# Rotary keys' low part: from 64 to 128 partitions

## The chip, the cores and the metric

The kernel runs on one core of one Trainium2 chip. The metric is the device time of one launch in microseconds (us). In the text, PE is TensorE (the matmul engine), DVE is VectorE, ACT is ScalarE, POOL is GpSimd, and SP the engine that issues most of the DMAs. SBUF and PSUM are the on-chip memories; matmuls write to PSUM. "Partitions" are the 128 rows of these memories, and for the two operands of a matmul they are the rows over which it sums.

## What is computed

Two layers over 512 latent tokens of width 1024, with 256 context tokens beside them. Layer 0 is a latent attention with 8 heads followed by a squared-ReLU MLP, layer 1 a gated MLP that mixes positions in chunks, followed by a second squared-ReLU MLP. The change lies in the attention's scores. Queries and keys have 128 entries without position and 64 rotary ones; the rotary part of the keys is one vector per token, shared by the heads, and only scaled by each head's norm:

```python
def mla_keys_values(h, wkv_a, kv_a_norm, wkv_b, k_norm):
    ...
    k_pe = jnp.broadcast_to(k_pe[:, :, None, :], (B, S, MLA_HEADS, QK_ROPE))
    k = rmsnorm(jnp.concatenate([k_nope, k_pe], axis=-1), k_norm)
    return k, v

def block_attention(q, k, v, scale):
    ...
        s = jnp.einsum('bqhd,bkhd->bhqk', qi, k, preferred_element_type=jnp.float32) * scale
        p = jax.nn.softmax(s, axis=-1)
        return jnp.einsum('bhqk,bkhd->bqhd', p.astype(v.dtype), v)
```

## The kernel before

Everything is float32 in memory, and matmuls run in a faster reduced form of it (`F32R`). To keep the precision, an operand is split in two: a high part, which is the value rounded to that form, and a low part, which is the rest (`split`, lines 70 to 77: ACT writes the high part, DVE or POOL subtracts). A product is then three matmuls: high by high, high by low, low by high (`mm3`, lines 79 to 82).

The attention goes head by head. For each head, `kv_proj` makes keys and values of all 768 tokens, `q_proj` makes the queries of two heads, `scores` makes the softmax of a half of the query tokens, `values` transposes the probabilities and multiplies them with the values, and `out_proj` multiplies the result with the output weights. These pieces are interleaved by a list of steps (`fill`), and the scheduler of the framework then sets the order on each engine; between `scores` and the `values` that use them lies other work, since the scores of a step are made one step ahead.

The rotary part of the queries is kept as one tile `sq` per head of 128 partitions: the high part on partitions 0 to 63 and the low part on 64 to 127, stacked. The rotary keys are transposed twice over, so that the same 64 rows stand on both halves of the PSUM tile `krt` (lines 536 to 541). From there ACT writes `rh`, the high part, on all 128 partitions (line 543), so that one product of `sq` with `rh` gives high by high plus low by high. DVE writes `rl`, the low part (line 544), on 64 partitions, and it is multiplied with partitions 0 to 63 of `sq` alone.

A score block, which is one pass through the loop on line 634, makes the scores of 128 queries of one head against 768 keys. It adds five products in PSUM (tile `s`, one buffer of two banks), each as two matmuls of 384 columns: ten matmuls on line 640. There are 32 blocks, 320 matmuls. A matmul here is two instructions on PE: one loads the stationary operand (`lhsT`, here the queries) into the array, listed as PEld, and one streams the other operand through it. A block's end releases DVE, which scales the scores and takes their maximum (line 644), then ACT the exponential (line 647), then DVE the division (line 649). The next block can't start before line 644 has read the tile.

While the attention runs, POOL also accumulates the modulation vectors (`ada_steps`, lines 169 to 172) from weights that it fetches itself.

Of the kernel before, what the change touches and what calls it, by code (L numbers as in the profile page):

```python
# [9 lines left out]
F32 = mybir.dt.float32  # L10
F32R = mybir.dt.float32r
BF16 = mybir.dt.bfloat16
AF = mybir.ActivationFunctionType
ALU = mybir.AluOpType
AX = mybir.AxisListType

P = 128
# [4 lines left out]
TOK = CTX + SEQ  # L22
# [4 lines left out]
ROPE = 64  # L27
# [19 lines left out]
def hybrid_dit_kernel(  # L47
# [7 lines left out]
    PE, ACT, DVE, POOL = nc.tensor, nc.scalar, nc.vector, nc.gpsimd  # L55
    SBUF, PSUM = bass.MemoryType.SB, bass.MemoryType.PSUM

    def pool(stack, name, bufs=1, space=SBUF, side="left"):
        return stack.enter_context(tc.tile_pool(name=name, bufs=bufs, space=space, side=side, reuse_waits="tile"))
# [157 lines left out]
    ap_ = pool(att, "att")  # L217
# [2 lines left out]
    cq_h = ap_.tile([P, 3, SEQ], F32R, name="cq_h")  # L220
    cq_l = ap_.tile([P, 3, SEQ], F32R, name="cq_l")
    rh = ap_.tile([P, TOK], F32R, name="rh")
    rl = ap_.tile([ROPE, TOK], F32R, name="rl")
    epk = ap_.tile([P, NT], F32, name="epk")
    cosT = ap_.tile([P, NT, ROPE], F32, name="cosT")
    sinT = ap_.tile([P, NT, ROPE], F32, name="sinT")
# [112 lines left out]
    with ExitStack() as ini_stack:  # L339
# [7 lines left out]
        def pt(name):  # L347
            return ps.tile([P, 512], F32, tag="t", bufs=2, name=name)

        def pa(name):  # L350
            return ps.tile([P, 512], F32, tag="a", bufs=6, name=name)
# [60 lines left out]
        with ExitStack() as xstack:  # L412
# [12 lines left out]
            for k in range(0, KT, 2):  # L425
                o = pa(f"xct{k}")
# [4 lines left out]
            for k in range(KT):  # L431
                o = pa(f"xt{k}")
# [7 lines left out]
        for t in range(NT):  # L440
            o = rp[0][:, t * P:(t + 1) * P] if t < 2 else rp[1][:, (t - 2) * P:(t - 1) * P]
# [18 lines left out]
        for k in range(KT):  # L460
# [6 lines left out]
            for t in range(NT):  # L467
                a_h, a_l = (ch, cl) if t < 2 else (hh[k], hl[k])
                s = bass.ts(t if t < 2 else t - 2, P)
# [23 lines left out]
        for t in range(NT):  # L493
# [8 lines left out]
            o = pt(f"ckt{t}")  # L502
            for j in range(2):
                PE.transpose(o[:, j * P:(j + 1) * P], ck[:, j * P:(j + 1) * P], ident)
            for j in range(2):
                s = slice(t * P, (t + 1) * P)
# [12 lines left out]
        for t in range(NL):  # L519
            o = pa(f"qa{t}")  # L520
            for k in range(KT):
                s = bass.ts(t, P)
# [15 lines left out]
        for u in range(2):  # L538
            o = pt(f"krt{u}")
            for j in range(3):  # L540
                PE.transpose(o[:, j * P:(j + 1) * P], kpe[:, 3 * u + j, :, :].rearrange("p a r -> p (a r)"), ident)
            s = slice(u * 384, (u + 1) * 384)
            ACT.copy(out=rh[:, s], in_=o[:, :384])
            DVE.tensor_tensor(out=rl[:, s], in0=o[:ROPE, :384], in1=rh[:ROPE, s].bitcast(F32), op=ALU.subtract)

        drain(kv0)

# [63 lines left out]
    with hst as st_:  # L611
# [17 lines left out]
        def scores(h, half):  # L629
            kh, kl, rk = Ks[h]  # L630
            rk = rk.rearrange("p (a b) -> p a b", a=2)
            qh, ql, sq, rq_ = Qs[h // 2]
            i = h % 2
            for t in (2 * half, 2 * half + 1):
                s = slice(t * P, (t + 1) * P)
                S = ps.tile([P, 2, 512], F32, tag="s", bufs=PS, name=f"s{h}{t}")
                ops = [(qh[:, i, s], kh), (qh[:, i, s], kl), (ql[:, i, s], kh), (sq[i][:, s], rh), (sq[i][:ROPE, s], rl)]
                for m, (a, b) in enumerate(ops):
                    for n in range(2):
                        PE.matmul(S[:, n, :384], lhsT=a, rhs=b[:, n * 384:(n + 1) * 384], start=m == 0, stop=m == 4)  # L640
                sm = hq.tile([P, 4], F32, tag="sm", bufs=4, name=f"sm{h}{t}")
                rq = rq_[:, t, i, 2:3]
                e = hq.tile([P, 2, 384], F32, tag="p", bufs=5, name=f"p{h}{t}")
                DVE.tensor_tensor_reduce(out=e, in0=S[:, :, :384], in1=rk, op0=ALU.mult, op1=ALU.max, scale=rq,  # L644
                                         scalar=-3.0e38, accum_out=sm[:, 0:1])
                DVE.tensor_scalar(out=sm[:, 1:2], in0=sm[:, 0:1], scalar1=-1.0, scalar2=None, op0=ALU.mult)  # L646
                ACT.activation(out=e, in_=e, func=AF.Exp, bias=sm[:, 1:2], accum_out=sm[:, 2:3])  # L647
                DVE.reciprocal(out=sm[:, 3:4], in_=sm[:, 2:3])
                DVE.tensor_scalar(out=e, in0=e, scalar1=sm[:, 3:4], scalar2=None, op0=ALU.mult)  # L649
                Pr[h, t] = e.rearrange("p a b -> p (a b)")  # L650
# [47 lines left out]
        drain(q_proj(0)); ada_step(8)  # L698
        steps = [(h, half) for h in range(HEADS) for half in range(2)]
        scores(0, 0)  # L700
        drain(kv_proj(1))
        fill = {}
# [7 lines left out]
        for i, (h, half) in enumerate(steps):  # L710
            if i + 1 < len(steps):
                scores(*steps[i + 1])
            values(h, half)
            ada_step(ADS[i])
            for g, n in fill.get((h, half), []):
                drain(g, n)
            if i == len(steps) - 2:
                out_last(3, 0)
# [117 lines left out]
    with ExitStack() as st_:  # L836
# [7 lines left out]
        for q in range(4):  # L844
            ws = [W(gm_w_in, 2 * k2, 2, HALF + q * 512, 512, f"gv{q}{k2}") for k2 in range(4)]
            for ts in ((0, 1), (2, 3)) if q == 0 else ((0, 1, 2, 3),):
                acc = {t: (pu if t < 2 else pd)(f"v{q}{t}") for t in ts}
                for k in range(KT):
                    wh, wl = ws[k // 2]
                    for t in ts:  # L850
                        s = slice(t * P, (t + 1) * P)
# [11 lines left out]
        for g4 in range(2):  # L863
            o = pt(f"wst{g4}")
# [6 lines left out]
            o = pt(f"rsw{g4}")  # L871
# [121 lines left out]
```

## Time and profile before

| | us |
|---|---|
| median of three runs | 1432.6 |
| the three runs | 1427.57, 1432.6, 1439.05 |
| the profiled execution | 1433.93 |
| its span (first to last instruction) | 1431.8 |
| PE busy in the span | 1370.9 (96%) |
| DVE busy | 872.3 (61%) |
| ACT busy | 547.3 (38%) |
| POOL busy | 243.8 (17%) |

The profile is that of one execution. A matmul's duration in it is the time from its start to a modelled end; matmuls overlap, so durations add up to more than the engine's time, and the distance from one start to the next tells the pace. A weight load (PEld) can overlap the matmul ahead of it. An idle stretch is given as "[0.25 <-issue]": so many us before the instruction, and what ended it, where "issue" means nothing that the profile shows. The granted clock is the share of the full clock of 2.4 GHz that PE had; 0.50 is 1.2 GHz.

### The profile page before, as it was taken

What the parts mean: (1) busy time and instruction counts of PE and PEld (TensorE: products, weight loads), DVE (VectorE), ACT (ScalarE), POOL (GpSimd) and SP (SyncE); (2) the same over time, 40 slices, a digit from 0 to 9 for tenths busy, and PEclk for the clock granted to TensorE, in tenths of its full rate; (3) what the DMA queues carried; (4) which work ended last, traced back from release to release, by engine and by line L of the source; (5) the groups of instructions that cost most, each with busy time, mean ns of one, the idle gap of its engine ahead of it and who ended that gap; (6) DMA issues with size and microseconds to landing.
All of it is one profiled execution on the core that took longest, in us unless ns stands there. A gap on an engine that the chain in (4) does not pass through costs nothing.

```text
span 1431.8 us, 18446 instructions
## 1 busy us (share of the span) xinstructions
PE 1370.9 (96%) x7159; PEld 1160.1 (81%) x7159; DVE 872.3 (61%) x1367; ACT 547.3 (38%) x1046; POOL 243.8 (17%) x262
## 2 busy tenths in 40 slices
PE   6887989999979999999999999999999999999998
PEld 4686878997868888888889788888888888888888
DVE  4766788778789988753456536555476344343443
ACT  6544654664454133231334423222245233242331
POOL 4467174173051111000000001000020000000000
PEclk9997999999989999999999999999999999999999
DMA  8523032131157888623232323222222233323311
GB/s 275 168 83 111 16 98 67 40 111 52 37 170 238 277 269 266 207 96 103 88 104 89 103 81 105 95 88 74 89 89 89 88 103 99 93 89 91 101 59 60
DMA packets 126823, 163.23 MB, mean 114 GB/s; under 512 B 7467, under 2 KB 111488, under 8 KB 126736
## 3 DMA queue, kind: packets, MB, share of 16 engines
q1 hardware_dynamic: 114784, 119.50, 26.4%
q0 software_dynamic: 11808, 42.03, 9.1%
q8 instruction: 56, 0.92, 0.3%
q10 hardware_dynamic: 144, 0.52, 0.1%
q14 instruction: 31, 0.25, 0.1%
HBM read 159.94 MB, written 2.10 MB: 113 GB/s over the span
## 4 chain that ended last, share of the span: by engine, by line
PE 86%; DVE 6%; ACT 2%; issue 1%; POOL 0%; DMA 0%; ACTq 0%; DVEq 0%; POOLq 0%
PE s L640 4%; PE v L80 2%; PE v L82 2%; PE v L81 2%; PE pt L662 1%; PE wo L80 1%; PE f1d2o L81 1%; PE f1d0o L80 1%; PE f1d0o L82 1%; PE f1d2o L82 1%; PE f1d2o L80 1%; PE f1d0o L81 1%; PE f0d0o L80 1%; PE f0d1o L80 1%; PE f0d1o L81 1%
## 5 line engine op out<-in xcount | busy, mean ns | idle before, releaser
L166 DVE SCALAR_TENSOR_TENSOR acc<-adr,sil,acc 128x1024 f32<-128x1024 f32 x49 | 62.8, 1281 | 9.5 <-DMA adr<-in_ada_w_dram 8.9
L161 POOL DMA_DIRECT2D adr<-in_ada_w_dram x80 | 44.0, 550 | 142.3 <-DVE acc L166 86.7
L172 POOL TENSOR_TENSOR acc<-acc,adr 128x512 f32<-128x512 f32 x42 | 55.7, 1343 | 0.2
L169 POOL TENSOR_TENSOR adr<-adr,sil 128x512 f32<-128x512 f32 x42 | 45.4, 1100 | 19.0 <-DMA adr<-in_ada_w_dram 19.0
L789 DVE TENSOR_TENSOR f1a<-f1a 128x512 f32<-128x512 f32 (+1 forms) x36 | 22.5, 629 | 41.3 <-ACT f1a L788 41.3
L644 DVE CUSTOM_DVE_ANT_0 p<-s,rk,rq 128x768 f32<-128x768 f32 x32 | 32.4, 1014 | 15.9 <-PE s L640 15.8
L126 POOL TENSOR_TENSOR nst<-nst,mhalf 128x2 f32<-128x2 f32 x6 | 4.6, 765 | 209.3 <-DVE nst L125 209.3
L73 DVE TENSOR_TENSOR tl<-pt,th 128x512 fp32r<-128x512 f32 x48 | 32.5, 685 | 11.3 <-ACT th L72 11.1
L72 ACT CAST f0uh<-f0a 128x512 fp32r<-128x512 f32 (+1 forms) x36 | 20.6, 573 | 48.5 <-DVE f0a L789 48.3
L789 DVE TENSOR_TENSOR f0a<-f0a 128x512 f32<-128x512 f32 (+1 forms) x36 | 22.6, 628 | 24.8 <-ACT f0a L788 24.8
L647 ACT ACTIVATE p<-p,sm 128x768 f32<-128x768 f32 x32 | 30.1, 940 | 15.6 <-DVE sm L646 15.4
L72 ACT CAST th<-pt 128x512 fp32r<-128x512 f32 x48 | 27.6, 588 | 20.2 <-PE o L82 11.6
L73 DVE TENSOR_TENSOR f1ul<-f1a,f1uh 128x512 fp32r<-128x512 f32 (+1 forms) x36 | 22.6, 631 | 18.7 <-ACT f1uh L72 18.5
L73 POOL TENSOR_TENSOR f1u00w01l<-f1u00w01r,f1u00w01h 128x1024 fp32r<-128x1024 f32 x1 | 2.4, 2390 | 182.0 <-ACT f1u00w01h L72 182.0
L72 ACT CAST f1uh<-f1a 128x512 fp32r<-128x512 f32 (+1 forms) x36 | 20.5, 572 | 32.8 <-DVE f1a L789 32.8
L81 PE MATMUL o<-tl,vh 128*128 128x256 f32 x96 | 28.5, 297 | 1.7 <-DVE tl L73 1.6
L73 DVE TENSOR_TENSOR f0ul<-f0a,f0uh 128x512 fp32r<-128x512 f32 (+1 forms) x36 | 22.6, 628 | 11.7 <-ACT f0uh L72 11.7
L649 DVE TENSOR_SCALAR p<-p,sm 128x768 f32<-128x768 f32 x32 | 29.0, 905 | 0.8
L80 PE MATMUL o<-th,vh 128*128 128x256 f32 x96 | 28.8, 300 | 0.0
L662 PE MATMUL pt<-ident,p 128*128 128x128 f32 x192 | 28.3, 276 | 0.0
L607 DVE SCALAR_TENSOR_TENSOR xT<-wo,mod,xT 128x512 f32<-128x512 f32 (+1 forms) x40 | 25.1, 638 | 4.0 <-PE wo L82 3.9
L82 PE MATMUL o<-th,vl 128*128 128x256 f32 x96 | 27.1, 282 | 0.0
(2640 smaller groups left out, 4815.3 us busy)
## 6 DMA issues: line engine op xcount, KB each, us to landing
adr<-in_ada_w_dram POOLq DMA_DIRECT2D x80, 512.0 KB, 4.8
xn<-in_x_dram SPq DMA_DIRECT2D x4, 512.0 KB, 7.1
out_dram<-of SPq DMA_DIRECT2D x8, 256.0 KB, 2.1
xn<-in_ctx_dram SPq DMA_DIRECT2D x2, 512.0 KB, 4.3
ada000r<-in_ada_w_dram SPq DMA_DIRECT2D x1, 512.0 KB
ada001r<-in_ada_w_dram SPq DMA_DIRECT2D x1, 512.0 KB
ada100r<-in_ada_w_dram SPq DMA_DIRECT2D x1, 512.0 KB, 11.2
ada101r<-in_ada_w_dram SPq DMA_DIRECT2D x1, 512.0 KB, 10.0
```

The lines of the kernel that those rows point to most:

```text
L72: ACT.copy(out=hi, in_=src)
L73: eng.tensor_tensor(out=lo, in0=src, in1=hi.bitcast(F32), op=ALU.subtract)
L80: PE.matmul(o, lhsT=wh, rhs=mh, start=start, stop=False)
L81: PE.matmul(o, lhsT=wh, rhs=ml, start=False, stop=False)
L82: return PE.matmul(o, lhsT=wl, rhs=mh, start=False, stop=stop)
L161: nc.gpsimd.dma_start(out=r, in_=ada_w[l][k * P:(k + 1) * P, ch * D:(ch + 1) * D])
L166: DVE.scalar_tensor_tensor(out=acc, in0=r, scalar=sil[:, k, 0:1], in1=acc, op0=ALU.mult, op1=ALU.add)
L169: POOL.tensor_tensor(out=(acc if k == 0 else r)[:, hf], in0=r[:, hf], in1=sil[:, k, 0:1].to_broadcast([P, D // 2]), op=ALU.mult)
L172: POOL.tensor_tensor(out=acc[:, hf], in0=acc[:, hf], in1=r[:, hf], op=ALU.add)
L640: PE.matmul(S[:, n, :384], lhsT=a, rhs=b[:, n * 384:(n + 1) * 384], start=m == 0, stop=m == 4)
L662: PE.transpose(T[:, j, q * P:(q + 1) * P], Pr[h, 2 * half + q][:, (2 * jp + j) * P:(2 * jp + j + 1) * P], ident)
L789: DVE.tensor_tensor(out=f, in0=f, in1=f, op=ALU.mult)
```

## The change

The tile `rl` gets 128 partitions instead of 64. The subtraction that fills it takes all partitions of the transposed tile and of `rh`, so the same 64 rows of low parts stand on both halves. The fifth product of a score block takes the whole stacked query tile with it, so that it sums over 128 rows instead of 64: high by low plus low by low, the last of which was not computed before.

```diff
-    rl = ap_.tile([ROPE, TOK], F32R, name="rl")
+    rl = ap_.tile([P, TOK], F32R, name="rl")
...
-            DVE.tensor_tensor(out=rl[:, s], in0=o[:ROPE, :384], in1=rh[:ROPE, s].bitcast(F32), op=ALU.subtract)
+            DVE.tensor_tensor(out=rl[:, s], in0=o[:, :384], in1=rh[:, s].bitcast(F32), op=ALU.subtract)
...
-                ops = [(qh[:, i, s], kh), (qh[:, i, s], kl), (ql[:, i, s], kh), (sq[i][:, s], rh), (sq[i][:ROPE, s], rl)]
+                ops = [(qh[:, i, s], kh), (qh[:, i, s], kl), (ql[:, i, s], kh), (sq[i][:, s], rh), (sq[i][:, s], rl)]
```

Every engine has the same number of instructions as before, in the same order; only the two subtractions and the 64 matmuls on `rl`, with their loads, have another shape.

## Rows read from the trace of the kernel before

**Rows 1.** Page, part 1: busy us, share of the span, instructions.

```profile
PE 1370.9 (96%) x7159; PEld 1160.1 (81%) x7159; DVE 872.3 (61%) x1367; ACT 547.3 (38%) x1046; POOL 243.8 (17%) x262
```

**Rows 2.** Stretches: length; PE, PEld, DVE, ACT, POOL busy (instructions); clock; DMA; GB/s.

```profile
142.00:380.00 238.00, 227.12 (x1438) 200.99 (x1439) 185.40 (x388) 130.67 (x370) 96.27 (x87) 0.98 0.20 62
182.40:185.60 3.20, 3.20 (x12) 3.20 (x11) 2.26 (x8) 2.25 (x7) 2.47 (x4) 0.50 0.41 118
```

**Rows 3.** Stretches, line 640 alone: length; PE, PEld busy (instructions); clock; DMA; GB/s.

```profile
142.00:380.00 238.00, 70.16 (x312) 51.44 (x312) 0.98 0.20 62
180.00:220.00 40.00, 9.26 (x42) 7.03 (x43) 0.91 0.28 88
300.00:340.00 40.00, 9.32 (x40) 6.34 (x38) 0.96 0.29 93
```

**Rows 4.** Chain that ended last, 142 to 380 us: shares by line; one piece.

```profile
by line: PE s L640 23.1%; PE pt L662 6.9%; PE wo L80 5.4%; PE wo L81 4.6%; PE wo L82 4.5%; PE o L81 4.2%; PE o L80 3.9%; PE kv L80 3.7%; PE o L82 3.7%; PE rkb L283 3.5%; PE kv L81 3.3%; PE kv L82 3.2%; PE q L80 2.6%; PE q L81 2.5%; PE q L82
...
375.59 1.94 PE s L640 x10
```

**Rows 5.** Waits of PE, 142 to 380 us: us in total, times, longest.

```profile
PE q L80 <- DVE qg L311: 2.9, 1, 2.9
```

**Rows 6.** Line 640 by operand: ns min/median/max, first and last start us.

```profile
L640 PEld LDWEIGHTS s<-rh,sq x64: 187/188/237, 141.2 to 376.5; 128*128 128x128 f32 x64
L640 PE MATMUL s<-rh,sq x64: 334/338/424, 141.4 to 376.6; 128*128 128x384 f32 x64
L640 PEld LDWEIGHTS s<-rl,sq x64: 182/183/187, 141.8 to 377.0; 64*128 64x128 f32 x64
L640 PE MATMUL s<-rl,sq x64: 327/436/442, 141.8 to 377.2; 64*128 64x384 f32 x64
```

**Rows 7.** PE in order of time, end of one block: start us, us taken.

```profile
376.12 0.51 PE L640 MATMUL s<-kh,ql 128*128 128x384 f32 x2
376.47 0.51 PE L640 MATMUL s<-rh,sq 128*128 128x384 f32 x2
376.91 0.44 PE L640 MATMUL s<-rl,sq 64*128 64x384 f32 x1
377.19 0.33 PE L640 MATMUL s<-rl,sq 64*128 64x384 f32 x1
377.46 0.38 PE L80 MATMUL wo<-oh,wo300h 128*128 128x256 f32 x1
377.68 0.28 PE L81 MATMUL wo<-ol,wo300h 128*128 128x256 f32 x1
377.80 0.28 PE L82 MATMUL wo<-oh,wo300l 128*128 128x256 f32 x1
```

**Rows 8.** Weight loads (PEld) in order of time, the same block.

```profile
376.30 0.36 PEld L640 LDWEIGHTS s<-rh,sq 128*128 128x128 f32 x2
376.91 0.29 PEld L640 LDWEIGHTS s<-rl,sq 64*128 64x128 f32 x2 [0.25 <-issue]
377.45 0.19 PEld L80 LDWEIGHTS wo<-oh,wo300h 128*128 128x128 f32 x1 [0.25 <-issue]
```

**Rows 9.** Waits of all engines, 142 to 380 us: total, times, longest.

```profile
PEld s L640 <- issue: 8.1, 33, 0.3
```

**Rows 10.** PE in order of time, at two other blocks.

```profile
145.95 0.66 PE L323 MATMUL qrt<-ident,qs 128*128 128x128 f32 x4
146.45 0.60 PE L272 MATMUL kt<-ident,kn 128*128 128x128 f32 x4
...
301.52 0.44 PE L640 MATMUL s<-rl,sq 64*128 64x384 f32 x1
```

**Rows 11.** DVE subtractions: line 544, and line 73 from 60 to 130 us.

```profile
L544 DVE TENSOR_TENSOR rl<-krt,rh x2: 536/538/541, 115.4 to 116.1; 64x384 fp32r<-64x384 f32 x2
...
L73 DVE TENSOR_TENSOR vl<-kv,vh x3: 411/424/425, 106.3 to 114.0; 128x256 fp32r<-128x256 f32 x3
```

**Rows 12.** Line 649 by tile p: ns min/median/max, first and last start.

```profile
L649 DVE TENSOR_SCALAR p<-p,sm x32: 610/621/3371, 148.0 to 380.7; 128x768 f32<-128x768 f32 x32
```

## Prediction

> **What bounds the kernel now.** I read the page first: TensorE (PE) is busy 96% of the span [rows 1]. That figure rests on modelled ends of overlapping matmuls, so it only says where to look. Then I took the stretch that holds the changed code. The score blocks (L640) run from 129 to 378 us. From 142 to 380 us PE is busy 227.1 of 238 us, VectorE (DVE) 185.4 of 238, that is 78%, and ScalarE and GpSimd (POOL) far less [rows 2]. So PE limits this stage, with DVE close enough behind it to take over in places. The chain that ended last, cut to the same stretch, says how much of the block lies on the path: 23.1% of 238 us, or 55 us, is L640 on PE [rows 4]. Of L640's 320 matmuls 312 fall in this stretch, so 31 of the 32 blocks [rows 3], and a whole one is a piece of 1.94 us on that chain [rows 4]; 31 × 1.94 = 60 us, so about 0.9 of the blocks' time is on the path. The rest lies beside waits: the longest wait that the list of waits puts down to another engine is 2.9 us, for DVE [rows 5].
>
> **What the 64-row product costs now.** The instructions themselves seem to say "nothing": the weight load of the 64-row product takes 183 ns against 188 ns for a full one [rows 6]. The median matmul differs, 436 against 338 ns [rows 6], but a duration of a pipelined matmul is not what it costs; what counts is the distance from one start to the next. That is read from one block, in order of time [rows 7]:
> - Inside the four full-width products two matmuls start every 0.35 us (376.12, 376.47), so 0.175 us each.
> - The second matmul on rh starts half of that after 376.47, at about 376.64; the first on rl starts at 376.91, that is 0.27 later: +0.095.
> - From the first on rl to the second, 376.91 to 377.19: 0.28 instead of 0.175, +0.105.
> - From the second on rl to the next instruction, 377.19 to 377.46: 0.27, +0.095.
> - From that instruction to the one behind it, 377.46 to 377.68: 0.22, where the same kind of pair, 256 columns wide, follows at 0.12 (377.68 to 377.80): +0.10.
>
> Together 0.395 us. Why is seen on the weight-load row of the same block [rows 8]: the two loads for rh start at 376.30, back to back in 0.36 us and ahead of their matmuls (376.47), while the matmul before still runs; the load of 64 rows starts only at 376.91, after a gap of 0.25 us that no semaphore accounts for, and the next full-width load has the same gap. Over the stage such gaps before L640's loads are 33, 8.1 us in all [rows 9], about one per block: the pipeline of load and matmul is emptied when the number of rows changes, and between the two narrow ones too.
>
> **Part by part.** (1) *The product.* All 320 matmuls of L640 become 128 rows by 384 columns. I take for the new pair the pace of the full-width products around it, 0.175 us, with loads under running matmuls. The four matmuls on rh and rl then read the same stationary tile, as the pair on rh does now at that pace. Saved: 0.395 us per block where a matmul follows. Where transposes follow, as in eight of the 32 blocks, the last term is smaller. Four transposes on L272 that follow other transposes take 0.60 us, the four on L323 right behind a block 0.66 [rows 10]: +0.06, so 0.355 per block. In three blocks the two matmuls on rl stand apart, with other work between them (one alone at 301.52 [rows 10]), and the way in and out is paid twice: 2 × 0.095 in and 2 × 0.195 out instead of 0.395, so 0.185 more. Sum on PE: 24 × 0.395 + 8 × 0.355 + 3 × 0.185 = 9.5 + 2.8 + 0.6 = 12.9 us. Should the new pair go no faster than the old, the sum is 0.
>
> (2) *The weight load* grows by 5 ns, 64 times, 0.3 us [rows 6], under the matmul before it; without that cover it would still be 0.3 us.
>
> (3) *The subtraction on L544* covers 128 partitions instead of 64, with 384 elements in each as before. The trace has no such form at full width. The nearest row at full width is the same subtraction out of PSUM over 256 elements, 424 ns against 538 for the 384 now [rows 11]. If all of its time grew with the elements, 384 would take 636: +0.1 each, 0.2 in all, once. If the partitions don't count, nothing; that row is the nearer, since going from 64 partitions by 384 to 128 by 256 made it shorter, so I take nothing.
>
> (4) *Order and queues.* No instruction is added, removed or moved on any engine, no DMA and no wait; the same instructions stand in the same order.
>
> What of the 12.9 reaches the end: 0.9 of it by the chain, 11.6. Where the chain is on DVE, PE only waits longer; and as PE gets ahead by some tenths per block, waits for DVE that are just not there now will appear. DVE's share of the stage rises from 78% to 185.4/226 = 82%. I take off 0.6 for them: **11.0 us**. The layers behind this stage start from its end and repeat the same instructions, so they pass the shift on. The profiled execution took 1433.9 us, 1.3 above the median of the three, 1432.6; 1433.9 − 11.0 = 1422.9 on its scale, **1422** at the median.
>
> **A rule against it.** The weight-load row shows full-width loads starting under full-width matmuls [rows 8]. The Trainium skill ("TensorE: Matmul & The Clock Gate", section on packing small matmuls, what overlaps and what doesn't) says that a load overlaps running matmuls only when their row groups differ. By that rule the full-width load, which shares its row groups with everything around it, would overlap no better than the narrow one and the sum would be 0 instead of 12.9. The trace does not agree with it here.
>
> **Rivals.**
> - *DVE takes the gain in the two tight places.* DVE instructions come out long at times: L649 takes 621 ns as a median and 3371 once [rows 12]. If two stretches of 40 us, from 180 and from 300 us, pass nothing on, their 82 matmuls of L640 fall out [rows 3], eight blocks: 12.9 × 24/32 × 0.9 is about 8.7, and less if new waits appear elsewhere; a gain of 4 to 8, so 1425 to 1429. For it: DVE's 78%. Against it: the factor 0.9 already leaves out what is hidden now.
> - *The switch isn't the cause.* If the slow starts came from the end of the accumulation or from the tile's place, not from the row count, the pace would stay and the time too: 1433. Against it: the first matmul on rl already starts late, and it ends no accumulation; and the load that waits out the gap is the narrow one [rows 8].
> - *Slower.* With the same order but other moments, more DVE instructions come out long; POOL, at work for 96.3 of the 238 us [rows 2], is my guess at what they meet. A long L649 costs up to 3.37 − 0.62 = 2.75 us [rows 12]. Five more of them on the path would be 14 us, 3 more than the gain: 1436. From the fifth on it decides: four cancel the gain. For it: the long one shows that it happens. Against it: an earlier start can as well remove one, and POOL's work is unchanged.
> - *More than the sum.* Three stretches of the stage, one of them from 182.4 to 185.6 us, show a granted clock of 0.50, that is 1.2 GHz instead of 2.4 [rows 2]. Half of such a stretch of some 3.2 us is lost, 1.6 us. If the moments fall so that two stretches and one long DVE instruction disappear, 3.2 + 2.75 = 6 more: 1416.
>
> **How the numbers follow.** Chances: the forecast, a gain of 9 to 13 (1420 to 1424), 0.62; DVE takes part of it 0.17; more than the sum 0.11; no change 0.05 (half of it by the rule above); slower 0.05. The three runs before spread by 11 us, so 1% (14.3 us) is about what can be told from no change. Faster by over 1%, under 1418.3, needs more than the whole PE sum: most of the fourth rival and a little of the forecast by spread, 0.16. Slower by over 1%, over 1446.9, would take more than nine of them, (14.3 + 11)/2.75: 0.02. Within 1%: 0.82. The range reaches from the fourth rival to the end of the first and its spread, 1416 to 1430; what is left out is no change, slower, and some of the tail on the fast side.
>
> **What would show it.** In the profile after: the L640 rows on rl read 128 x 384 with a median near 338 ns; a whole block runs at 0.175 us per start through its last matmul and what follows it; the 0.25 us gaps on the weight loads and the 8.1 us "issue" row are gone; L640's share of the chain falls by about a fifth. That is right even if the time hardly moves. The forecast is wrong on the path if PE's idle time for DVE in this stage grows by more than 2 us, or if the long DVE instructions change in number; it is wrong on the cause if the narrow starts go but 0.27 us stays.

## The result, and the profile after

| | before | after |
|---|---|---|
| median of 14 runs, us | 1433.2 | 1421.9 |
| lowest to highest | 1427.5 to 1439.1 | 1417.1 to 1431.5 |
| the profiled execution | 1433.93 | 1428.05 |
| its span | 1431.8 | 1425.9 |

The ratio is 0.9933, 95% interval 0.9916 to 0.995: 0.67% faster, 9.6 us by the ratio (7.2 to 12.0 by its interval); the two medians lie 11.3 us apart. The forecast was a gain of 11.0 us and 1422 us, and "within 1%" as the likeliest class.

Line 640 by operand, of the kernel after (ns min/median/max, first and last start, forms), against [rows 6]:

```profile
L640 PEld LDWEIGHTS s<-rl,sq x64: 187/188/189, 142.3 to 366.8; 128*128 128x128 f32 x64
L640 PE MATMUL s<-rl,sq x64: 333/338/419, 142.5 to 367.0; 128*128 128x384 f32 x64
```

The product on rl now looks like the one on rh did before. The same block as in [rows 7], PE in order of time (start us, us taken):

```profile
366.11 0.51 PE L640 MATMUL s<-kh,ql 128*128 128x384 f32 x2
366.46 0.51 PE L640 MATMUL s<-rh,sq 128*128 128x384 f32 x2
366.80 0.51 PE L640 MATMUL s<-rl,sq 128*128 128x384 f32 x2
367.15 0.29 PE L80 MATMUL wo<-oh,wo300h 128*128 128x256 f32 x1
367.28 0.28 PE L81 MATMUL wo<-ol,wo300h 128*128 128x256 f32 x1
```

Every pair takes 0.35 us from start to start, the one on rl too, and the two instructions behind the block start 0.13 apart. From the first matmul on ql to the second instruction behind the block it was 377.68 − 376.12 = 1.56 us; it is 367.28 − 366.11 = 1.17, that is 0.39 less. The same subtraction can be made in every block, at the two starts on rl and the two behind each, since both kernels have the same instructions in the same order: the median over the 32 blocks is 0.38 us less, and all of them together make 13.3 us. The weight loads of the same block, against [rows 8], have no gap left:

```profile
366.29 0.36 PEld L640 LDWEIGHTS s<-rh,sq 128*128 128x128 f32 x2
366.63 0.36 PEld L640 LDWEIGHTS s<-rl,sq 128*128 128x128 f32 x2
366.98 0.19 PEld L80 LDWEIGHTS wo<-oh,wo300h 128*128 128x128 f32 x1
```

The row of [rows 9], 33 gaps with 8.1 us, has no counterpart in the waits of after. The subtraction on line 544 took 543 ns against 538 [rows 11].

The gain is where it was looked for. The second and the last score block start here, first of before, then of after (start us):

```profile
143.92 0.34 PE L640 MATMUL s<-kh,qh 128*128 128x384 f32 x1
...
375.42 0.34 PE L640 MATMUL s<-kh,qh 128*128 128x384 f32 x1
```

```profile
144.26 0.42 PE L640 MATMUL s<-kh,qh 128*128 128x384 f32 x1
...
365.41 0.34 PE L640 MATMUL s<-kh,qh 128*128 128x384 f32 x1
```

Between them lie 231.50 us before and 221.15 after: 10.35 less, over 30 blocks. The profiled execution of after nevertheless gained only 5.9 us in its span. It is 10.4 us ahead behind the last block and still 9.8 us ahead at 1047 us; the 3.9 us between that and 5.9 went in one place far from the change, at the start of the second MLP. Stretches there (length; PE, PEld, DVE, ACT, POOL busy; clock; DMA; GB/s), first of before, then of after:

```profile
1055.00:1085.00 30.00, 28.02 (x240) 27.48 (x238) 25.78 (x57) 17.00 (x37) 8.99 (x5) 1.00 0.23 71
```

```profile
1056.60:1063.20 6.60, 5.96 (x28) 5.96 (x29) 6.60 (x16) 3.62 (x8) 0.00 (x0) 0.50 0.28 96
```

In this one execution PE had 1.2 GHz for 6.6 us there, and before had 2.4 GHz. Just ahead of that stretch PE waited 1.9 us for ACT (line 598), a wait that the kernel before does not show there; what made it is open. Single executions differ in such spells: this one, 1428.05 us, had a mean granted clock of 0.979, one of 1417.54 us had 0.985. The medians are the measure, not the two spans.

### The profile page after: what moved, and what is told of

It reads as the page before. It is cut to its first block, busy times and chain, and to the rows that moved or that the text cites. A ratio compares the mean times of both kernels' runs of the same rounds, so it can differ in the third digit from the quotient of the medians.

```text
span 1425.9 us, 18446 instructions
## 1 busy us (share of the span) xinstructions
PE 1358.9 (95%) x7159; PEld 1163.3 (82%) x7159; DVE 875.5 (61%) x1367; ACT 546.4 (38%) x1046; POOL 242.2 (17%) x262
## 4 chain that ended last, share of the span: by engine, by line
PE 75%; DVE 10%; DMA 5%; issue 4%; ACT 2%; POOL 1%; DVEq 0%; POOLq 0%; ACTq 0%
DMA adr<-in_ada_w_dram 4%; PE s L640 3%; PE v L80 2%; PE v L82 2%; PE v L81 2%; PE pt L662 1%; PE f1d2o L82 1%; PE f1d0o L81 1%; PE f1d0o L80 1%; PE f1d2o L81 1%; PE f1d2o L80 1%; PE f1d0o L82 1%; PE f1d1o L81 1%; PE f0d2o L81 1%; PE f0d2o L82 1%
## 5 line engine op out<-in xcount | busy, mean ns | idle before, releaser
L789 DVE TENSOR_TENSOR f1a<-f1a 128x512 f32<-128x512 f32 (+1 forms) x36 | 22.5, 629 | 41.3 <-ACT f1a L788 41.3
L649 DVE TENSOR_SCALAR p<-p,sm 128x768 f32<-128x768 f32 x32 | 30.3, 948 | 0.8
```

Source lines behind the costliest of these rows:

```text
L789: DVE.tensor_tensor(out=f, in0=f, in1=f, op=ALU.mult)
```

## Experiments

All times are medians, and each ratio is to runs of the kernel before on the same chip. Each rival was to be told apart by the time and by the starts on PE.

**Half of the change: the tile without the product.** The edit is made on the changed kernel.

```diff
-... (sq[i][:, s], rh), (sq[i][:, s], rl)]
+... (sq[i][:, s], rh), (sq[i][:ROPE, s], rl[:ROPE])]
```

> Half of the change alone: rl lies on 128 partitions and line 544 fills them all, but the fifth product still sums over the first 64 rows. Every engine keeps its order. If the number of rows in the matmul is the cause: the first matmul on rl again starts 0.27 us behind the one before, 0.28 between the two, 0.27 behind them, and the time is that of the kernel before within 0.3%, about 1433 us; line 544 takes at most 0.1 us more. If the place of rl (64 or 128 partitions of memory) were the cause, the gain of 11 us would be here already: about 1422.

Measured: 1432.9 us, ratio 0.9995 (0.9979 to 1.001). PE in order of time at the last block, where the second matmul on rh starts at 372.34:

```profile
372.61 0.44 PE L640 MATMUL s<-rl,sq 64*128 64x384 f32 x1
...
372.89 0.33 PE L640 MATMUL s<-rl,sq 64*128 64x384 f32 x1
373.15 0.38 PE L80 MATMUL wo<-oh,wo300h 128*128 128x256 f32 x1
```

These are the starts of before: 0.27, 0.28 and 0.26 us apart. Line 544 took 543 ns with all partitions. So the tile and the subtraction bring no gain that the runs can tell from nothing, and the gain lies in the row count of the product.

**Another place: the narrow product second.**

```diff
-ops = [(qh[:, i, s], kh), (qh[:, i, s], kl), (ql[:, i, s], kh), (sq[i][:, s], rh), (sq[i][:ROPE, s], rl)]
+ops = [(qh[:, i, s], kh), (sq[i][:ROPE, s], rl), (qh[:, i, s], kl), (ql[:, i, s], kh), (sq[i][:, s], rh)]
```

> The kernel before with the narrow product moved from fifth to second place in the block; the full-width product on rh ends it. If the row count is the cause: the same four late starts (0.27, 0.28, 0.27, and the second start behind it late by 0.10) now stand at the block's second product, and the end of the block runs at 0.175 us; time within 0.5% of before (the scheduler shifts some blocks, so the time may move by some us either way). If the end of the accumulation or the last place is the cause: the late starts stay at the end of the block, now on rh, and the narrow product in second place runs at 0.175.

Measured: 1434.4 us, ratio 1.0011 (0.9994 to 1.0028). PE in order of time at one block:

```profile
374.49 0.51 PE L640 MATMUL s<-kh,qh 128*128 128x384 f32 x2
374.93 0.62 PE L640 MATMUL s<-rl,sq 64*128 64x384 f32 x2
375.47 0.62 PE L640 MATMUL s<-kl,qh 128*128 128x384 f32 x2
375.93 0.51 PE L640 MATMUL s<-kh,ql 128*128 128x384 f32 x2
376.28 0.51 PE L640 MATMUL s<-rh,sq 128*128 128x384 f32 x2
376.63 0.28 PE L80 MATMUL wo<-oh,wo300h 128*128 128x256 f32 x1
```

The late starts moved along: 0.44, 0.54 and 0.46 us from pair to pair around the narrow product instead of 0.35, and 0.35 at the end of the block. The rival "the end of the accumulation or the tile's place" falls.

**Twice as many changes of the row count.**

```diff
-for m, (a, b) in enumerate(ops):
-    for n in range(2):
+for m, n in [(0, 0), (0, 1), (1, 0), (1, 1), (2, 0), (2, 1), (3, 0), (4, 0), (3, 1), (4, 1)]:
+    a, b = ops[m]
...
```

> The kernel before with rl narrow, its last four matmuls of each block in another order: rh, rl, rh, rl instead of rh, rh, rl, rl. Same work, but the row count changes in and out twice per block. If a change of the row count is what costs (0.095 us in, 0.195 out): 0.58 us per block instead of 0.395, 0.185 x 32 = 5.9 us more on PE, about 5 of it in the time: 1438, 0.35% slower. If each narrow matmul has a fixed extra price whatever stands beside it: the same 0.395 per block and the time of before, 1433.

Measured: 1444.4 us, ratio 1.0082 (1.0056 to 1.0108), some 11 us slower, where 5 were expected. PE at the last block:

```profile
387.10 0.34 PE L640 MATMUL s<-rh,sq 128*128 128x384 f32 x1
387.36 0.44 PE L640 MATMUL s<-rl,sq 64*128 64x384 f32 x1
387.73 0.44 PE L640 MATMUL s<-rh,sq 128*128 128x384 f32 x1
388.10 0.43 PE L640 MATMUL s<-rl,sq 64*128 64x384 f32 x1
388.47 0.38 PE L80 MATMUL wo<-oh,wo300h 128*128 128x256 f32 x1
388.69 0.28 PE L81 MATMUL wo<-ol,wo300h 128*128 128x256 f32 x1
```

A single full-width matmul between two narrow ones takes 0.37 us from start to start, and a single narrow one too. That is 0.19 over the 0.175, at each change of the row count. It doesn't fit a price of 0.095 for the way in, 0.195 for the way out and 0.105 between narrow ones; it fits 0.19 for any change, half of it at the first instruction of the new kind (0.26 or 0.27 where the one before it had no change behind it) and half at the next (388.47 to 388.69 is 0.22, where 0.12 is the undisturbed step [rows 7]). Four changes cost 0.77 us per block (387.10 to 388.69 is 1.59, undisturbed it would be 4 × 0.175 + 0.12 = 0.82), against 0.39 for two.

**One narrow matmul instead of two.** The edit is made on the changed kernel.

```diff
-for n in range(2):
-    PE.matmul(S[:, n, :384], lhsT=a, rhs=b[:, n * 384:(n + 1) * 384], ...)
+for n, g in enumerate((slice(0, ROPE), slice(0, P)) if m == 4 else [slice(0, P)] * 2):
+    PE.matmul(S[:, n, :384], lhsT=a[g], rhs=b[g, n * 384:(n + 1) * 384], ...)
```

> From the changed kernel, same order on all engines: of the two matmuls on rl in a block the first sums over 64 rows, the second over 128. One way in and one way out per block, no two narrow ones in a row. If a change of the row count costs 0.095 us in and 0.195 out and two narrow neighbours 0.105 on top: 0.29 per block, 9.3 us more on PE than the changed kernel, some 8 in the time: 1430, between the two. If each narrow matmul has its own fixed price (half of 0.395): 6.3 more on PE, 5.5 in the time: 1427.

Measured: 1432.8 us, ratio 0.9987 (0.9974 to 1.0001): no gain over the kernel before that can be told from nothing, where the two theories expected 1430 and 1427. By the time alone 1430 lies at the edge of the interval; the starts decide. The two matmuls of the fifth product, the first narrow, the second full:

```profile
372.75 0.44 PE L640 MATMUL s<-rl,sq 64*128 64x384 f32 x1
...
373.12 0.44 PE L640 MATMUL s<-rl,sq 128*128 128x384 f32 x1
...
373.39 0.28 PE L80 MATMUL wo<-oh,wo300h 128*128 128x256 f32 x1
```

The starts are 0.27 apart on the way in (the pair on rh starts at 372.31, its second matmul at 372.48), then 0.37, then 0.27: with the two narrow ones it was the same 0.39 us above 0.175 each. That is two changes of the row count, two times 0.19; whether one narrow matmul lies between them or two makes no difference.

**Four narrow matmuls in a row**, as a test of that, on the kernel before.

```diff
-... (sq[i][:, s], rh), (sq[i][:ROPE, s], rl)]
+... (sq[i][:ROPE, s], rh[:ROPE]), (sq[i][:ROPE, s], rl)]
```

> The kernel before with the fourth product narrow too: rh is taken with partitions 0 to 63 alone (this leaves out the low part of the queries by the high part of the rotary keys), so four narrow matmuls stand in a row at the block's end. Same order on all engines. New theory from the earlier runs: a change of the row count costs 0.19 us, 0.095 at the first instruction of the new kind and 0.10 at the one behind it; narrow neighbours cost nothing more. Then starts of 0.27, 0.28, 0.175, 0.175, 0.265 and 0.10 extra behind, 0.39 per block as before: 1433. The theory of the prediction (two narrow neighbours cost 0.105 each time) gives 0.21 more per block, 6.7 on PE, about 6 in the time: 1439.

Measured: 1432.4 us, ratio 0.9997 (0.9975 to 1.0018). PE at the last block:

```profile
373.28 0.44 PE L640 MATMUL s<-rh,sq 64*128 64x384 f32 x1
...
373.56 0.33 PE L640 MATMUL s<-rh,sq 64*128 64x384 f32 x1
373.73 0.34 PE L640 MATMUL s<-rl,sq 64*128 64x384 f32 x1
...
374.16 0.39 PE L80 MATMUL wo<-oh,wo300h 128*128 128x256 f32 x1
```

The second narrow matmul starts 0.28 behind the first, the third 0.17 behind the second: narrow neighbours run at the pace of full ones once the change is over. The time is that of before, not the 1439 of the prediction's theory. The new theory holds, and the prediction's "between the two narrow ones too" falls.

**The two narrow matmuls in different halves.** The edit is made on the changed kernel.

```diff
-for n in range(2):
+for n, g in enumerate((slice(0, ROPE), slice(ROPE, P)) if m == 4 else [slice(0, P)] * 2):
...
```

> From the changed kernel, same order on all engines: the fifth product is 64 rows again, but its first matmul (keys 0 to 383) takes partitions 0 to 63 and its second (keys 384 to 767) partitions 64 to 127, so neighbours lie in different halves of the array. For keys 384 to 767 it leaves out the high part of the queries by the low part of the keys (it has low by low instead). If the load can be hidden where the two narrow ones lie in different rows: from the first to the second 0.175 us or less instead of 0.28, so 0.105 x 32 = 3.4 us less on PE than before, 1430; side by side in the array up to 0.28 x 32 = 9 less, 1425. If any narrow load waits for the matmul before it: 0.28 stays, and the time is that of before, 1433.

Measured: 1429.2 us, ratio 0.9969 (0.9952 to 0.9985).

```profile
371.82 0.51 PE L640 MATMUL s<-rh,sq 128*128 128x384 f32 x2
372.26 0.44 PE L640 MATMUL s<-rl,sq 64*128 64x384 f32 x2
372.63 0.39 PE L80 MATMUL wo<-oh,wo300h 128*128 128x256 f32 x1
```

Both matmuls together take 0.44 us, as one does alone: they run side by side, and the next instruction starts 0.37 behind the pair. The two changes are still paid. What is saved is the stream of one matmul, 0.175 us per block, 32 × 0.175 = 5.6 us, of which 4.4 arrived by the ratio. The Trainium skill ("TensorE: Matmul & The Clock Gate", section on packing small matmuls) says that matmuls addressed to different tiles of the array run concurrently. The trace agrees: the pair takes no longer than one. It isn't worth as much as having no change at all, 9.6 us.

**POOL's share in DVE's delays.** The prediction guessed that POOL makes DVE instructions long. POOL's work was cut down in both kernels, the one before ("narrow") and the changed one ("full"); with the cut their instructions still stand in the same order. The weights that POOL works on are fetched whole as before.

```diff
-for hf in (slice(0, D // 2), slice(D // 2, D)):
+for hf in (slice(0, D // 2), slice(D // 2, D)) if k == 0 else (slice(0, 8),):
...
```

> The kernel before, with POOL's accumulation of the modulation vectors in the attention cut down: for seven of eight weight tiles only 8 of the 1024 columns are multiplied and added (so three modulation vectors are not the right ones). If POOL is what makes DVE instructions come out long: L649's maximum falls from 3.37 us to about its median of 0.62, the 20 long DVE instructions of the attention (together 23 us too long) nearly vanish, and PE's waits for DVE with them: 5 to 10 us faster than before, 1423 to 1428. If they have another cause, they stay, and the time too.

> The changed kernel with the same cut of POOL's accumulation (same vectors not right). Against the narrow kernel with the same cut, whose order on all engines is the same, it tells how much of PE's 12.9 us passes when DVE is not held up: if DVE's long instructions absorb the missing part, nearly all, 12 to 13 us; if something else absorbs it, again 10 to 11.

Measured: 1406.7 us narrow, ratio 0.981 (0.9796 to 0.9825), and 1392.8 us full, 0.9715 (0.9699 to 0.973). For the narrow one 1423 to 1428 was expected, so the cut brought more than was looked for. The row on the division, narrow with the cut, against [rows 12] (the cut adds a line to the kernel, so line 649 is line 650 here):

```profile
L650 DVE TENSOR_SCALAR p<-p,sm x32: 610/621/1508, 136.3 to 358.2; 128x768 f32<-128x768 f32 x32
```

The longest division falls from 3.37 to 1.51 us, and of PE's waits for another engine between 132 and 360 us four are left, of 1.8, 0.9, 0.3 and 0.2 us. In the kernel before, that longest one starts at 226.66 and runs beside POOL's additions (first DVE, then POOL, start us, us taken):

```profile
226.66 3.37 DVE L649 TENSOR_SCALAR p<-p,sm 128x768 f32<-128x768 f32 x1
```

```profile
227.07 2.54 POOL L172 TENSOR_TENSOR acc<-acc,adr 128x512 f32<-128x512 f32 x2
```

The other DVE instructions say the same. Call one late if it took over 0.3 us more than the median of its kind (same line, tiles and shape). Between the first and the last score block of the kernel before 19 are late, 22.5 us together, and each of them overlaps work of POOL; with the cut one is left, 0.9 us late. The cut also changed the order that the scheduler chose, so the 27 us are not all shown to be delays of DVE; that DVE's late instructions go away with POOL's work is.

How much of PE's gain passes then? The second and the last block, narrow with the cut, then full with the cut (line 640 is 641 here):

```profile
132.18 0.34 PE L641 MATMUL s<-kh,qh 128*128 128x384 f32 x1
...
352.66 0.42 PE L641 MATMUL s<-kh,qh 128*128 128x384 f32 x1
```

```profile
128.53 0.42 PE L641 MATMUL s<-kh,qh 128*128 128x384 f32 x1
...
338.43 0.42 PE L641 MATMUL s<-kh,qh 128*128 128x384 f32 x1
```

Between the two starts lie 220.48 and 209.90 us: 10.6 less, as against 10.35 without the cut. So no more of the gain passes when DVE is not late, as far as one execution of each can tell. The medians of the two kernels differ by 13.9 us, 3 more than the stage; in these two executions 3.7 us lie ahead of the second block (132.18 against 128.53), 3.3 of them already at 87 us, in code that the change doesn't touch; the cause stays open.

**POOL in other pieces.** POOL's two operations were cut to quarters, eighths and whole tiles, on the changed kernel, and to quarters on the kernel before:

```diff
-for hf in (slice(0, D // 2), slice(D // 2, D)):
+for hf in [slice(q * D // 4, (q + 1) * D // 4) for q in range(4)]:
...
```

> The changed kernel with POOL's accumulation in quarters of 256 columns instead of halves of 512: the same sums in twice as many instructions. If a DVE instruction is held up until the POOL instruction that it meets is over, the hold-ups get shorter: L649's maximum falls towards 2 us, the sum of the excess from 24 to some 12 to 16 us, and the time by 2 to 5 us against the changed kernel: 1417 to 1420. If the hold-up is as long as POOL's whole work whatever its pieces, or POOL gets slower by its fixed cost per instruction, the same time or a few us more: 1422 to 1426.

> The kernel before with POOL's accumulation in quarters of 256 columns; its order on all engines is that of the changed kernel with quarters (1410.7 us), so the two differ by the change alone. If DVE's hold-ups beside POOL absorbed the missing part of PE's gain: with them shorter, 12 to 13 us between the two, so 1423. If they don't matter for it, 10 to 11.5: 1421 to 1422. Against the kernel before: 10 to 12 us faster, as the quarters brought on the changed kernel.

> The changed kernel with POOL's accumulation in eighths of 128 columns. If the hold-up of a DVE instruction ends with the POOL instruction that it meets: L649's maximum from 1.16 us (quarters) to under 0.9, and the time at or a few us under that of quarters, 1405 to 1411, unless POOL's fixed cost per instruction makes its vectors late. If the gain of the quarters came from the other order of the instructions and not from shorter hold-ups, no further gain, 1411 or more.

> The changed kernel with POOL's accumulation in whole tiles of 1024 columns, the other direction. If the length of the POOL instruction sets the hold-up: L649's maximum to 4 us and more, the excess of the long DVE instructions from 24 to 35 us or more, and 5 to 15 us slower than the changed kernel: 1427 to 1437. If only the order matters, no trend: 1411 to 1422.

Late is meant as above, between the first and the last score block of one execution:

| kernel | us | ratio to before (95%) | longest L649, us | DVE late, us |
|---|---|---|---|---|
| changed, whole tiles | 1421.0 | 0.9900 (0.9870 to 0.9931) | 2.55 | 26.7 |
| changed, halves (the change) | 1421.9 | 0.9933 (0.9916 to 0.9950) | 3.26 | 26.9 |
| changed, quarters | 1410.7 | 0.9837 (0.9817 to 0.9858) | 1.16 | 11.5 |
| changed, eighths | 1414.0 | 0.9856 (0.9822 to 0.9890) | 5.63 | 7.0 |
| before, quarters | 1414.3 | 0.9869 (0.9834 to 0.9903) | 1.20 | 8.0 |

Quarters beat both kernels, and by more than was expected of them (1417 to 1420 on the changed kernel, 1421 to 1423 on the one before). But neither the time nor the longest division follows the length of POOL's pieces: whole tiles were not slower, and eighths had the longest division of all (first DVE, then POOL, in order of time):

```profile
190.67 5.63 DVE L649 TENSOR_SCALAR p<-p,sm 128x768 f32<-128x768 f32 x1
```

```profile
192.14 3.75 POOL L172 TENSOR_TENSOR acc<-acc,adr 128x128 f32<-128x128 f32 x9
```

POOL's pieces took 0.39 to 0.46 us each there. So a delay doesn't end with the one POOL instruction that DVE meets, and that theory falls. What does fall from halves on is the sum of the delays; the time does not follow it all the way, since eighths were not faster than quarters. Each cut also gave the scheduler's order another shape; how much of the 11 us between halves and quarters is order and how much is delay was not told apart.

The two kernels with quarters ran on different chips, each beside the kernel before. Their ratios differ by 0.0032, some 4.6 us, but with 6 and 4 runs that does not tell 9.6 us from nothing. The stage itself shows the change again: from the second block to the last 357.79 − 134.75 = 223.04 us narrow, and 356.46 − 143.21 = 213.25 full, 9.8 less. What these two executions lose on the other side comes ahead of the second block, 8.5 us (134.75 against 143.21). There PE waits 3.4 us for a late result of DVE (ql) and 2.9 us for another (wkb1l) with quarters and full width; narrow shows the second alone, with 0.6 us.

## Why the prediction held, step by step

- *The price per block*, 0.395 us, was right: 0.39 in the block shown, with the same follower, and 0.34 to 0.35 where transposes follow, against the 0.355 of the prediction. The starts that gave it were the right view; the durations (436 against 338 ns) and the load times (183 against 188) would have led elsewhere.
- *The split of that price* was wrong. The step "and between the two narrow ones too" read the second late start as a cost of two narrow neighbours. It is the second half of the price of the first change: a change costs 0.19 us, 0.095 at the first instruction of the new kind and 0.10 at the next, and there are two changes per block. The same holds for the 0.195 that the prediction counted as the way out. For the change made here both readings give the same sum. For two experiments they don't, and there the expectations failed: with one narrow matmul 0.39 remains instead of 0.29, and with four changes 0.77 comes instead of 0.58. The term for the three split blocks was too small for the same reason: 2 × 2 changes each, 0.79, 0.76 and 0.74 us measured instead of the 0.58 counted, 0.6 us in all. With it the sum would have been 13.5 instead of 12.9; measured on PE were 13.3.
- *That it lies in the row count*: shown, by the half change (0.9995) and by the narrow product in second place. It is not that the new pair reads the same stationary tile as the one on rh: from ql to sq, two different tiles, the pairs start 0.35 us apart too (376.12 to 376.47 [rows 7]).
- *The subtraction and the weight load*, taken at nothing: 543 against 538 ns, and 188 against 183, the load under the matmul before it.
- *What reaches the end*. The factor from the chain, 0.9, and 0.6 off for new waits gave 11.0 of 12.9, that is 0.85. By the ratio 9.6 of the 13.3 us saved on PE arrived, 0.72, and its interval reaches from 0.54 to 0.90; so the factor is not contradicted, and how close the forecast came to the medians is in part luck. The stage gave 10.35 us over 30 of the 32 blocks, where PE saved 12.5 at the starts that the change touches and lost 2.2 elsewhere. One execution can't settle that either: with the same order and the same price per block the kernels with the half change, with one narrow matmul and with four took 229.95, 229.58 and 229.81 us for this stretch, not the 231.50 of before, and against them the stage gains 8.4 to 8.8. Waits are where the rest went. The waits of PE for another engine, first two of before (142 to 380 us; the longest is in [rows 5]), then all of after (142 to 372 us):

```profile
PE qt L314 <- DVE qn L310: 2.4, 1, 2.4
...
PE wo L80 <- DVE xT L607: 0.9, 1, 0.9
```

```profile
PE wo L80 <- DVE xT L607: 4.0, 2, 3.1
PE o L81 <- DVE tl L73: 3.1, 3, 2.1
PE q L80 <- DVE qg L311: 2.9, 1, 2.9
PE kv L80 <- DVE vl L73: 2.2, 1, 2.2
PE s L640 <- DVE sm L644: 1.0, 1, 1.0
```

They sum to 13.2 us; the whole list before sums to 10.9, that is 2.3 more, all for DVE, and about as much as PE lost outside the changed starts. The prediction had named two signs that its path was wrong, a growth of over 2 us and another number of long DVE instructions. Both came: among DVE's instructions in the blocks 24 are late instead of 19 (of the divisions 8 in both). The first sign was set too tight, since the sum itself had taken 1.9 us off. Whether DVE's delays beside POOL cause these waits is open: with POOL's work cut the stage passed 10.6 us on, hardly more.
- *The chain*: L640 went from 23.1% of 238 us, 55 us, to 19.7% of 230, 45 us. Its time on the chain fell by 18% and its share by 15%, where a fall of the share by about a fifth was forecast.

```profile
by line: PE s L640 19.7%; PE pt L662 6.5%; DVE p L649 4.6%; DVE qtm L238 4.3%; PE o L81 4.0%; PE wo L80 4.0%; PE wo L82 3.8%; issue 3.7%; PE o L82 3.7%; PE wo L81 3.7%; PE o L80 3.5%; PE kv L80 3.2%; PE kv L81 3.2%; PE kv L82 3.2%; PE rkb L
```

- *The rivals.* That DVE took no more than the factor allowed fits the medians, but the interval, 7.2 to 12.0 us, does not exclude a part of that rival. "More than the sum" and "slower" did not come as medians, but their mechanisms do move single executions by several us, as the spell at 1056.6 us shows. The rule that a full-width load wouldn't overlap full-width matmuls would have left the time as it was; it does not hold here: the loads on rl start 0.17 us ahead of their matmuls, under the one before.

## What to carry to other kernels

A product that sums over 64 rows among products over 128 costs 0.19 us at each change of the row count, with the 384 columns of this kernel. The load doesn't show it (183 against 188 ns), and the matmul's duration shows something else (436 against 338 ns); the starts show it. Fill the product up to the rows of its neighbours with data that does no harm, or put the narrow products next to each other, so that the changes are paid once. Read the price of a matmul from the distance to the next start, over the two instructions behind a change and not one. In this kernel, with PE at 95% of the stage and DVE near 80%, some 0.7 of the saving on PE reached the end (0.54 to 0.90); a pair of single executions is too coarse to find such a share.

## What was not expected of the hardware

- The price of a change between 128 and 64 rows falls on two instructions, 0.095 and 0.10 us, and is the same into 64 rows and out of them; a single matmul between two changes takes 0.37 us from start to start instead of 0.175.
- Two 64-row matmuls in different halves of the partitions, written one behind the other, ran side by side without any further step: the pair took 0.44 us, a single one 0.44 (376.91 in [rows 7]).
- A DVE division of 0.62 us took up to 5.63 us while POOL was working, twelve times as long as one of POOL's pieces there (0.39 to 0.46 us). Every late DVE instruction between the score blocks of before and after overlaps work of POOL.
